# Rotary embedding in a two-block network: the half swap by ScalarE copies out of PSUM or by DMA transfers inside SBUF

## The chip, the cores and the metric

The kernel runs on one core of one Trainium2 chip. The metric is the time of one execution on the device, in microseconds. A core has five engines that run side by side, each through its own queue in order: TensorE (PE; its weight loads are listed as PEld), VectorE (DVE), ScalarE (ACT), GpSimd (POOL) and SyncE (SP). SBUF is the core's working memory of 128 partitions, PSUM the memory that TensorE writes its sums to, and 16 DMA engines move data to and within SBUF.

## What is computed

The reference is a network of two blocks over 256 tokens of 1,024 features, batch 1. The first block has two attention layers, one with compressed, selected and windowed keys and one with dilated windows; the second block has a gated feed-forward part, a mixer with a gated delta rule and a convolution, and a second feed-forward part. All is float32. What matters here is the rotary embedding, which is applied to heads of 64 features in both attention layers:

```python
def rope(x):
    T = x.shape[1]
    half = x.shape[-1] // 2
    inv = ROPE_THETA ** (-jnp.arange(half, dtype=jnp.float32) / half)
    ang = jnp.arange(T, dtype=jnp.float32)[:, None] * inv[None, :]
    cos = jnp.cos(ang)[None, :, None, :]
    sin = jnp.sin(ang)[None, :, None, :]
    xf = x.astype(jnp.float32)
    x1, x2 = xf[..., :half], xf[..., half:]
    return jnp.concatenate([x1 * cos - x2 * sin, x2 * cos + x1 * sin], axis=-1).astype(x.dtype)
```

Each output needs the feature of its own place and the feature of the other half of its head.

## The kernel before

Activations lie transposed: features on the partitions, 128 at a time (a feature tile), and the 256 tokens along the row. A feature tile holds two heads of 64, so the halves of the heads are four blocks of 32 partitions, and to change the halves means that block 0 goes to block 1, 1 to 0, 2 to 3 and 3 to 2.

All products with weights stream the weights once from memory. A unit of up to 1 MB comes by one DMA from SP into one of three buffers named raw (`fetch`, line 234). To keep float32 accuracy at the speed of a reduced format, it is cut into a high part `hi` (a cast on ACT, line 216) and a low part `lo` (a subtraction on DVE, line 219), and PE makes three passes for each pair of tiles. The raw buffer is free again when the subtraction has read it. Beside this, `ada_gen` makes the modulation sums of later layers on DVE (line 371) out of further units of raw, at a rate that the code sets per stage.

A group of 512 output columns fills two PSUM banks, each with two feature tiles of 256 tokens. PSUM has three banks tagged g, two s, two t and one o. When a group is complete, an evacuation function takes the banks out. For q and k these are:

- `ev_kv` and `ev_q` in the first attention layer (lines 754 and 774). `ev_kv` copies the bank to a temporary on ACT (line 760) and calls `rope` once; `ev_q` scales the bank into `qp` on ACT (line 777) and calls `rope` for each of four banks. What comes out is cut into high and low parts (lines 766, 783, 784) for the scores.
- `ev_r` in the second attention layer (line 988). It scales the bank into a temporary on ACT (line 991) and calls `rope`, for four banks of q and four of k. The results go straight to `qr` and the block-diagonal `kr`, from which `scores` (line 1011) starts as soon as the k of four head pairs is there.

So `rope` runs 13 times. It gets the scaled values twice: `src` in SBUF, and the bank `ps` in PSUM with the factor `scale`. Four ACT instructions (line 677), one for each block of 32 partitions, read the neighbouring block of the bank, scale it and write it to a temporary `t2`; DVE multiplies that with the signed sine (line 678); POOL multiplies `src` with the cosine (line 680); DVE adds both (line 682). The temporaries [128, 512] (tag w5) have four buffers for all uses. In the second layer a call holds three: the scaled copy, `t2` and the cosine product. In the first layer it holds `t2`, the cosine product and the result.

Within an engine the order of instructions is fixed when the program is built: a planner goes through the program with its own estimate of durations, takes what is ready by priority, and places the waits between engines. At run time each engine works through its list in that order.

Of the kernel before, what the change touches and what calls it, by code (L numbers as in the profile page):

```python
# [14 lines left out]
PSUM = bass.MemoryType.PSUM  # L15
# [97 lines left out]
FILL = [[1, 2, 0, 0, 0, 0, 0], [1, 1, 2, 0, 0, 2, 2]]  # units of the queued products at the seven points of a half of the delta rule  # L113


def pack_small(inp):
    """Vectors as columns: element q of row r of the row-major [rows, 128] view goes to (q, r)."""
# [9 lines left out]
def pack_w2(inp):  # L127
    """Second compression matrices, their 64 columns twice: [128, k/v, k tile, 128]."""
    two = [np.concatenate([np.asarray(inp[f"nsa_c{n}_w2"])[0].reshape(2, 128, 64)] * 2, 2).transpose(1, 0, 2) for n in "kv"]
    return np.ascontiguousarray(np.stack(two, 1))  # L130
# [10 lines left out]
def pack_units(inp, plan):  # L141
    """Weights in the order and layout in which the kernel reads them, 128 partitions by up to 2048 words a unit."""
# [15 lines left out]
class Net:  # L158
# [20 lines left out]
    # ------------------------------------------------------------ helpers  # L179
# [12 lines left out]
    def touch(self, t):  # L192
        """Slots of a tag are given out in the order of the first writes: this takes one now for a tile filled later."""
        self.nc.gpsimd.memset(t[:, 0:1].bitcast(F32), 0.0)
        return t
# [35 lines left out]
    # ------------------------------------------------------------ weights  # L231
# [25 lines left out]
    def group(self, ncol, orient="A", tags="ggg", tail=False, wide=False):  # L257
        """Accumulators for at most 512 columns of a weight: banks, place of each tile in them, tiles, first matmuls"""
# [9 lines left out]
    def direct(self, G, ws, x, k0, nkt):  # L268
        """Adds the float32 products of feature tiles k0 on with the weights as they came."""
# [15 lines left out]
    def part(self, G, ws, act, k0, nkt, early=False, late=False, passes=((0, 0), (1, 0), (0, 1))):  # L285
        """Adds the products of feature tiles k0 on, whose weights are ws, to a group."""
# [27 lines left out]
    def fill(self, n):  # L314
        """The next n units of the products that wait to be put between the steps of others."""
# [4 lines left out]
    def until(self, gen):  # L320
        """All units of a product that waits."""
# [3 lines left out]
    def gemm_steps(self, wsrc, cols, act, evac, orient="A", tail=False, last=None, x=None, dset=()):  # L325
        """cols = list of (c0, width) forming one group of at most 512 columns of the weight.
        A: evac(bank list, each [128, 2, 256] = feature tiles); B: evac([bank per token tile])."""
# [31 lines left out]
    # ------------------------------------------------------------ background modulation sums  # L359
# [30 lines left out]
    # ------------------------------------------------------------ setup  # L390
    def setup(self):
# [20 lines left out]
        # modulation jobs in the order of their need  # L412
# [23 lines left out]
    def silu_row(self, row, pe=False):  # L436
        """silu of a vector, in every partition"""
# [20 lines left out]
    # ------------------------------------------------------------ norm  # L458
    def stats(self, xT, k0, n, two=False):
        """Adds feature tiles k0 to k0 + n of x to the sums of squares per token; two: also to those weighted by self.og."""  # L460
# [22 lines left out]
    def rstd(self):  # L483
        """1 / rms over features, in every partition: PSUM [128, 256]."""
# [6 lines left out]
    def spread(self, r, tag):  # L491
        """A value per token, [128, 2], in every partition: PSUM [128, 256]."""
# [5 lines left out]
    def normed(self, xT):  # L498
        """hi/lo of rms_norm(x) * g * (1 + scale) + shift, per feature tile, and the first products."""
# [5 lines left out]
    def ahead(self, g, mod, j, g0=None):  # L505
        """The factor and the shift of the norm that follows a projection, known before its sums of squares are."""
# [8 lines left out]
    def unscaled(self):  # L515
        """The first columns behind a norm: (r * a * x + s) @ w = r * ((a * x) @ w) + s @ w, so that the product with w
        doesn't wait for r.  s goes along as two more tokens, its high and its low part."""
# [15 lines left out]
    def rescaled(self):  # L533
        """The feature tiles of these columns, [128, 512] for two."""
# [1129 lines left out]
```

## Time and profile before

| | us |
|---|---|
| median of the timed runs | 1123.79 |
| lowest and highest of them | 1122.24, 1124.45 |
| span of the profiled execution | 1131.5 |
| PE busy | 1077.3 |
| DVE busy | 861.2 |
| ACT busy | 616.7 |
| POOL busy | 64.4 |

The profile is of one execution, recorded instruction by instruction; its span is from the first to the last instruction. Busy times of an engine count its instructions and not the issue of DMAs. PE's matmuls are pipelined, so a busy PE is not PE at its peak. Where an engine sat idle, the profile names what ended the wait. An idle engine costs time only if something that sets the end waits for it.

### The profile page before, as it was taken

What the parts mean: (1) busy time and instruction counts of PE and PEld (TensorE: products, weight loads), DVE (VectorE), ACT (ScalarE), POOL (GpSimd) and SP (SyncE); (2) the same over time, 40 slices, a digit from 0 to 9 for tenths busy, and PEclk for the clock granted to TensorE, in tenths of its full rate; (3) what the DMA queues carried; (4) which work ended last, traced back from release to release, by engine and by line L of the source; (5) the groups of instructions that cost most, each with busy time, mean ns of one, the idle gap of its engine ahead of it and who ended that gap; (6) DMA issues with size and microseconds to landing.
All of it is one profiled execution on the core that took longest, in us unless ns stands there. A gap on an engine that the chain in (4) does not pass through costs nothing.

```text
span 1131.5 us, 20245 instructions
## 1 busy us (share of the span) xinstructions
PE 1077.3 (95%) x8145; PEld 1003.1 (89%) x8145; DVE 861.2 (76%) x1571; ACT 616.7 (55%) x1190; POOL 64.4 (6%) x70
## 2 busy tenths in 40 slices
PE   5889999989999999999999799999999999999997
PEld 4868776977789899999989679998999999999997
DVE  7885887799999898887689789568866667565543
ACT  3482676688765644444388246644644556444442
POOL 0030000222000000000000020002000000000000
PEclk9998999999999999999999989999999999999998
DMA  8855455657768487878743523263346544555451
GB/s 332 330 202 198 149 172 201 247 207 258 259 240 292 178 316 266 310 271 326 261 153 139 147 76 114 81 220 113 117 145 227 184 152 176 195 178 177 169 185 38
DMA packets 33423, 226.34 MB, mean 200 GB/s; under 512 B 3681, under 2 KB 3937, under 8 KB 7346
## 3 DMA queue, kind: packets, MB, share of 16 engines
q1 hardware_dynamic: 32914, 224.20, 55.0%
q8 instruction: 64, 1.05, 0.4%
q10 hardware_dynamic: 288, 0.52, 0.1%
q0 software_dynamic: 128, 0.33, 0.1%
q14 instruction: 29, 0.24, 0.1%
HBM read 223.73 MB, written 1.31 MB: 199 GB/s over the span
## 4 chain that ended last, share of the span: by engine, by line
issue 35%; PE 20%; DVE 6%; DMA 3%; ACT 2%; POOL 1%; SPq 0%; POOLq 0%; DVEq 0%; ACTq 0%
PE g L206 12%; PE s L206 5%; DMA b<-dr 2%; DVE w L1218 1%; DVE lo L219 1%; PE t L206 1%; DMA raw<-in_ws_dram 1%; PE o L206 1%; ACT hi L216 1%; DVE xt L1368 0%; POOL rrq L1279 0%; PE t L213 0%; DVE xs L1369 0%; DVE b L1447 0%; DVE b L1456 0%
## 5 line engine op out<-in xcount | busy, mean ns | idle before, releaser
L206 PE MATMUL g<-b,hi 128*128 128x256 f32 (+2 forms) x3696 | 692.2, 286 | 9.1 <-ACT b L586 7.3
L206 PEld LDWEIGHTS g<-b,hi 128*128 128x128 f32 (+1 forms) x3696 | 578.7, 191 | 16.5 <-ACT b L586 9.2
L206 PE MATMUL g<-b,lo 128*128 128x256 f32 (+2 forms) x1848 | 520.1, 286 | 8.6 <-DVE lo L219 8.5
L216 ACT CAST hi<-raw 128x1024 fp32r<-128x1024 f32 (+2 forms) x302 | 280.1, 953 | 228.6 <-PE g L206 124.6
L219 DVE TENSOR_TENSOR lo<-raw,hi 128x1024 fp32r<-128x1024 f32 (+2 forms) x302 | 328.5, 1110 | 90.7 <-ACT hi L216 90.3
L206 PEld LDWEIGHTS g<-b,lo 128*128 128x128 f32 (+1 forms) x1848 | 348.8, 191 | 12.6 <-DVE lo L219 10.3
L371 DVE SCALAR_TENSOR_TENSOR raw<-raw,scrow 128x1024 f32<-128x1024 f32 x120 | 147.1, 1247 | 4.0 <-DMA raw<-in_ws_dram 3.9
L206 PE MATMUL s<-b,hi 128*128 128x256 f32 (+1 forms) x288 | 63.8, 288 | 2.3 <-ACT w L546 2.3
L206 PE MATMUL g<-b,raw 128*128 128x256 f32 x208 | 52.3, 385 | 0.0
L206 PE MATMUL s<-b,b 128*128 128x128 f32 (+2 forms) x224 | 49.0, 342 | 3.0 <-DVE b L682 1.5
L206 PEld LDWEIGHTS s<-b,hi 128*128 128x128 f32 x288 | 49.4, 193 | 2.5 <-ACT w L546 2.5
L1218 DVE SCALAR_TENSOR_TENSOR w<-pad,u,w 128x256 f32<-128x256 f32 x96 | 41.7, 481 | 2.3 <-ACT w L1213 2.2
L206 PEld LDWEIGHTS g<-b,raw 128*128 128x128 f32 x208 | 37.2, 191 | 5.0 <-issue 0.5
L206 PE MATMUL s<-b,lo 128*128 128x256 f32 (+1 forms) x144 | 40.4, 288 | 0.0
L206 PEld LDWEIGHTS s<-b,b 128*128 128x128 f32 x224 | 30.2, 191 | 8.2 <-ACT b L1028 3.2
L206 PE MATMUL t<-b,hi 128*128 128x256 f32 x160 | 37.4, 280 | 0.0
L1129 DVE TENSOR_TENSOR w<-w,g 128x512 f32<-128x512 f32 (+1 forms) x21 | 14.2, 675 | 24.8 <-PE g L206 24.8
L925 ACT ACTIVATE p<-s,mxs 128x256 f32<-128x256 f32 (+1 forms) x64 | 26.4, 420 | 9.5 <-DVE mxs L923 7.0
L488 POOL TENSOR_TENSOR rcol<-rcol,u 128x2 f32<-128x2 f32 x5 | 3.5, 702 | 489.4 <-ACT rcol L487 489.4
L1127 ACT ACTIVATE w<-g 128x512 f32<-128x512 f32 (+1 forms) x21 | 12.3, 587 | 33.0 <-PE g L206 33.0
L206 PE MATMUL g<-hi,b 128*128 128x512 f32 (+1 forms) x96 | 28.2, 372 | 1.8 <-ACT hi L216 1.6
L206 PEld LDWEIGHTS o<-u,w 128*128 128x128 f32 x224 | 27.4, 192 | 1.2 <-issue 0.6
(321 smaller groups left out, 1323.8 us busy)
## 6 DMA issues: line engine op xcount, KB each, us to landing
raw<-in_ws_dram SPq DMA_DIRECT2D x202, 1024.0 KB, 4.8
b<-dr SPq DMA_DIRECT2D x8, 512.0 KB
raw<-in_ws_dram SPq DMA_DIRECT2D x4, 512.0 KB, 3.8
raw<-in_ws_dram SPq DMA_DIRECT2D x2, 608.0 KB, 3.9
b<-in_xT_dram SPq DMA_DIRECT2D x1, 1024.0 KB
u<-in_consts_dram SPq DMA_DIRECT2D x2, 384.0 KB
u<-in_consts_dram SPq DMA_DIRECT2D x1, 527.0 KB
u<-in_consts_dram SPq DMA_DIRECT2D x2, 256.0 KB, 5.9
```

The source lines that it names most:

```text
L206: i = self.nc.tensor.matmul(out, lhsT=lhsT, rhs=rhs, start=start, stop=stop, skip_group_check=True)
L216: i = self.nc.scalar.copy(hi, src)
L219: self.nc.vector.tensor_tensor(lo, src, hi, op=ALU.subtract)
L371: nc.vector.scalar_tensor_tensor(r, r, 1.0, sc, op0=ALU.mult, op1=ALU.mult, accum_out=mod[:, n:n + 1])
L488: nc.gpsimd.tensor_tensor(r, r, self.mhalf[:, 0:2], op=ALU.pow)
L925: nc.scalar.activation(p[:, br], sv[:, br], AF.Exp, bias=mx[:, q, br:br + 1], accum_out=den[:, q, br:br + 1])
L1127: nc.scalar.activation(t, gb, AF.Tanh, scale=0.5)
L1129: nc.vector.tensor_tensor(t, t, ub, op=ALU.mult)
L1218: nc.vector.scalar_tensor_tensor(dst, fl(pad[:, o:o + 256]), taps[i], dst, op0=ALU.mult, op1=ALU.add)
```

## The change

In `rope` the four ACT copies out of PSUM are replaced by four DMA transfers from `src`, the scaled values in SBUF. They are issued on ACT's queue, and each moves 32 partitions by 512 float32 values (64 KB). The parameters `ps` and `scale` stay in the signature and are no longer used. All other lines of the diff are comments and docstrings that became empty lines.

```diff
         t2 = v(self.w([128, 512], tag="w5", bufs=4))
         for k in range(4):
-            nc.scalar.activation(t2[32 * k:32 * k + 32], ps[32 * (k ^ 1):32 * (k ^ 1) + 32], AF.Copy, scale=scale)
+            nc.scalar.dma_start(t2[32 * k:32 * k + 32], src[32 * (k ^ 1):32 * (k ^ 1) + 32])
         nc.vector.tensor_tensor(t2, t2, bc("ropes"), op=ALU.mult)
```

With it `t2` waits for `src` to be written and for its buffer, the bank `ps` is read by one ACT instruction (in `ev_kv` by that one and the copies of line 759), and line 678 waits for four transfers. ACT still issues the step, from its own queue, and SP's queue has nothing new in it.

## Rows read from the trace of the kernel before

**Rows 1.** The page's first part: busy us, share of the span, instructions.
```profile
PE 1077.3 (95%) x8145; PEld 1003.1 (89%) x8145; DVE 861.2 (76%) x1571; ACT 616.7 (55%) x1190; POOL 64.4 (6%) x70
```
**Rows 2.** By stretch: PE, PEld, DVE, ACT, POOL busy (instructions), clock, DMA share, GB/s.
```profile
50.00:92.00 42.00, 37.06 (x234) 29.64 (x234) 34.33 (x55) 32.10 (x59) 9.94 (x7) 0.93 0.58 209
225.00:300.00 75.00, 69.12 (x429) 57.00 (x429) 70.25 (x101) 62.13 (x140) 13.51 (x8) 1.00 0.65 226
92.00:225.00 133.00, 130.12 (x808) 104.22 (x807) 100.02 (x242) 80.21 (x238) 5.72 (x7) 0.96 0.54 195
300.00:570.00 270.00, 268.17 (x2201) 261.26 (x2199) 227.67 (x393) 135.85 (x202) 2.57 (x6) 1.00 0.74 274
```
**Rows 3.** Waits in 225 to 300: who for whom, us, times, longest.
```profile
DVE w L678 <- ACT w L677: 3.4, 5, 1.6
...
PE g L206 <- ACT w L677: 1.1, 2, 1.0
```
**Rows 4.** Waits in 50 to 92 us.
```profile
PE o L206 <- DMA raw<-in_ws_dram: 2.0, 2, 1.6
...
PE g L206 <- ACT hi L216: 1.6, 1, 1.6
...
DVE w L678 <- ACT w L677: 0.5, 1, 0.5
```
**Rows 5.** Line 677: count, ns min/median/max, first and last start.
```profile
L677 ACT ACTIVATE w<-g x36: 588/590/593, 54.1 to 280.3; 32x512 f32<-32x512 f32 x36
...
L677 ACT ACTIVATE w<-w x4: 625/628/632, 232.1 to 234.0; 32x512 f32<-32x512 f32 x4
```
**Rows 6.** Line 621, the stores at the end: issue ns, and landing.
```profile
L621 SPq DMA_DIRECT2D out_dram<-b x2: 338/345/352, 1126.5 to 1127.7; - x2
L621 ACTq DMA_DIRECT2D out_dram<-b x2: 338/356/374, 1127.1 to 1128.3; - x2
...
DMA to landing us min/median/max: 2.1/2.2/2.2
```
**Rows 7.** DMA issues with size and us to landing; then issue ns of line 1352.
```profile
raw<-in_ws_dram SPq DMA_DIRECT2D x202, 1024.0 KB, 4.8
w<-in_w_dram SPq DMA_DIRECT2D x1, 256.0 KB, 4.2
...
L1352 SPq DMA_DIRECT2D b<-dr x8: 567/572/697, 619.3 to 740.1; - x8
```
**Rows 8.** DVE's groups in 225 to 300: busy us, mean ns, idle before.
```profile
L219 DVE TENSOR_TENSOR lo<-raw,hi 128x1024 fp32r<-128x1024 f32 (+1 forms) x20 | 23.8, 1223 | 0.7 <-ACT hi L216 0.7
L371 DVE SCALAR_TENSOR_TENSOR raw<-raw,scrow 128x1024 f32<-128x1024 f32 x14 | 19.1, 1376 | 0.0
L1025 DVE TENSOR_REDUCE dmx<-s 128x2 f32<-128x256 f32 (+1 forms) x16 | 8.6, 553 | 0.1
```
**Rows 9.** ACT in order of time, first layer: start us, us.
```profile
69.11 1.79 ACT L677 ACTIVATE w<-s 32x512 f32<-32x512 f32 x3
70.93 0.95 ACT L216 CAST hi<-raw 128x912 fp32r<-128x912 f32 x1
```
**Rows 10.** PE in order of time; in brackets idle before it, and its releaser.
```profile
71.93 0.55 PE L206 MATMUL g<-hi,b 128*128 128x304 f32 x2 [1.63 <-ACT hi L216]
```
**Rows 11.** Busy time by stretch, 65 to 80 us (columns as in rows 2).
```profile
65.00:70.00 5.00, 3.42 (x17) 1.68 (x16) 4.18 (x6) 4.82 (x9) 1.57 (x2) 1.00 0.76 261
70.00:75.00 5.00, 2.98 (x10) 1.14 (x8) 4.12 (x5) 4.84 (x9) 2.00 (x1) 0.81 0.69 249
75.00:80.00 5.00, 5.00 (x28) 4.02 (x27) 3.62 (x8) 4.56 (x8) 1.29 (x1) 0.85 0.39 118
```
**Rows 12.** ACT in order of time, second layer, from one scaled copy to the next.
```profile
239.72 0.60 ACT L991 ACTIVATE w<-g 128x512 f32<-128x512 f32 x1
240.35 2.39 ACT L677 ACTIVATE w<-g 32x512 f32<-32x512 f32 x4
242.77 0.60 ACT L991 ACTIVATE w<-g 128x512 f32<-128x512 f32 x1
```

## The prediction

> **What bounds the kernel now.** I read the page's busy shares first. TensorE (PE) is busy 95% of the profiled span, DVE 76%, ACT 55% [rows 1]. So the time is PE's work plus PE's gaps, and the 31 us that ACT spends on these copies are worth nothing unless a gap of PE, or of an engine that PE waits for, hangs on them. The next view is busy time by stretch [rows 2]. The 13 calls of rope lie in two stretches: five in 50 to 92 us (one for k, four for q of the first layer) and eight in 225 to 300 us (four for q, four for k of the second). There PE has 4.9 and 5.9 us of gaps. In the second stretch DVE is busy 70.25 of 75 us, so it is nearly the bound beside PE; in the first, DVE is at 34.3 and ACT at 32.1 of 42. After each stretch PE is close to full (130.1 of 133, 268.2 of 270), so what is lost or won in a rope stretch is mostly carried to the end.
>
> The third view is the waits of both stretches. What the four copies of line 677 hold up today is little: DVE's product with the sine (line 678) waits 3.4 us in five places of the second stretch and 0.5 us in the first, and PE waits 1.1 us for the copies to give back an accumulator bank [rows 3, 4]. The longest gap of PE in the first stretch that has ACT behind it is 1.6 us for a weight cast of line 216 [rows 4].
>
> **What is removed.** 52 ScalarE copies: 36 out of the g banks at 0.59 us, 12 out of other banks at the same 0.59, and 4 from SBUF at 0.63 [rows 5] (the first and the last of four groups); 52 x 0.59 = 31 us of ACT. A group of four reads 2.40 us in order of time [rows 12], so a rope loses 2.40 us of ACT.
>
> **What is added.** 52 transfers of 32 partitions by 2,048 bytes, 64 KB each, issued on ACT's queue. The only DMAs issued there now are two stores of 256 KB at 0.356 us of ACT's sequencer; the cheapest of the four stores took 0.34 on SP [rows 6], and the dearest group of issues, b<-dr, 0.57 [rows 7]. I take 0.356: 4 x 0.356 = 1.42 us a rope. ACT keeps 2.40 - 1.42 = 0.98 us a rope, 12.7 us in all (bounds 2.40 - 4 x 0.57 = 0.1 to 2.40 - 4 x 0.34 = 1.0 a rope).
>
> **How late the swapped halves are.** Today they are there 2.4 us after the scaled copy. A transfer's time to landing is not shown for this size, nor for SBUF to SBUF. From below: 2.1 us, the stores on the quiet queue at the end [rows 6]. From above: 4.2 us for a 256 KB load inside the first rope stretch, 4.8 for a full 1 MB load [rows 7]. The DMA engines are 58% and 65% busy in the two stretches [rows 2], so I weigh quiet and busy by 0.35 and 0.65: 0.35 x 2.1 + 0.65 x 4.2 = 3.5 us. The last of four is issued 3 x 0.356 = 1.07 us after the first, so the halves are there after 4.6 us (bounds 1.07 + 2.1 = 3.2 and 1.07 + 4.8 = 5.9): 2.2 us later than now.
>
> The Trainium skill, "DMA: Bandwidth & Descriptors", section "Queues, rings and completion order", says that a DMA engine takes turns between its queues packet by packet, so these transfers would not stand behind a whole weight load. By that, a rope's transfers wait only for about their own volume of weights: 768 KB more take a load 4.8 - 2.1 = 2.7 us longer [rows 6, 7], so 256 KB take 0.9, the halves would come after 3.2 + 0.9 = 4.1 us (an estimate by that rule), and the sum below would be +0.6 in place of +1.4 us. No row here shows two loaded queues side by side.
>
> **Who waits.** Behind line 678 DVE's whole in-order queue is held: the subtractions of line 219 that give PE its low weights, the modulation sums of line 371, the score maxima of line 1025. That queue also has what can cover the wait: 23.8 + 19.1 + 8.6 = 51.5 us of such work in the second stretch [rows 8], 6.4 us a rope. The order is made at build time, and today it leaves uncovered 3.4 of 8 x 2.4 = 19.2 us (18%) in the second stretch and 0.5 of 12 us (4%) in the first. I keep these shares for the longer latency: 0.18 x 8 x 4.6 = 6.6 and 0.04 x 5 x 4.6 = 0.9, together 7.5 us of DVE waiting in place of 3.9: **+3.6 us**. If everything is covered it is -3.9; if 40% of the second stretch is not, 14.7 + 0.9 - 3.9 = +11.7.
>
> **What PE wins.** The bank is free after the first copy and not after five ACT instructions, so the 1.1 us that PE waits for line 677 go [rows 3]. The cast that PE waits 1.63 us for starts at 70.93, right behind copies of line 677 that run from 69.11 [rows 9, 10]; three ropes' savings (3 x 0.98) are ahead of it, so that wait goes too, and the weight load of the compression is next in line. Together **-2.7 us** (bounds 0 and -2.7, and a little of clock: the gaps from 65 to 75 us are followed by a granted clock of 0.81 and 0.85 up to 80 us, part of that time at 1.2 instead of 2.4 GHz; were it all given back it would be 5 x 0.19 + 5 x 0.15 = 1.7 us [rows 11]).
>
> **What the weight loads lose.** A rope moves 256 KB, a quarter of a 1 MB load, so by the load's time it can set a load back by up to 4.8 / 4 = 1.2 us. PE waits for loads only at the compression, 2.0 us in two places [rows 4]: 0 to 2.4 us. The engines are idle 35 to 42% of the time, so most of it finds room; I take **+0.5 us**. SP's own queue is passed by nothing, since ACT issues the transfers; POOL's product with the cosine (line 680) reads the same source as before and is unmoved.
>
> **Sum.** +3.6 - 2.7 + 0.5 = +1.4 us. It is made on a profiled execution with a span of 1131.5 us; the timed runs have a median of 1123.79 (1122.24 to 1124.45), 7.7 us under that span, so I carry the difference over: 1123.79 + 1.4 = **1125.2 us**. With U for the uncovered DVE wait the net is U - 3.9 - 2.7 + 0.5 = U - 6.1.
>
> **The rivals.** About 0.2% (2.25 us) is what a measurement of this kernel can tell from no change. By the line above, U under 3.85 us (0.30 a rope) is faster, over 8.35 us (0.64 a rope) slower.
>
> Slower, by DVE: the order puts line 678 where it thinks the halves have landed, and beside weight loads they have not. At 40% uncovered in the second stretch, where DVE has under 5 us of slack, the net is 15.6 - 6.1 = +9.5 us, 1133. For it: DVE is 94% busy there, and the DMA engines are busier (65%) than where the 4.2 us landing was (58%). Against it: 51.5 us of other DVE work to hide 37 us of latency in.
>
> Slower, by ACT's queue: the pool of [128, 512] temporaries has four buffers, and a rope of the second layer holds three (scaled copy, swapped, cosine product). The swapped tile of the second rope of a pair must take the buffer of the first rope's scaled copy, which the transfers now read until they land. ACT reaches its issue 0.60 + 1.42 = 2.0 us after the first copy's end and would stand until 4.6: 2.6 us, for four pairs 10.3 us, with casts of line 216 behind it [rows 12]. ACT's slack (12.9 us plus 7.8 saved) takes most; if one of the holds reaches PE and the wins are lost too, 1.4 + 2.7 + 2.6 = +6.7, 1130.5.
>
> Slower, by transfers one behind the other: four landings in a row take 4 x 2.1 = 8.4 us, U = 0.18 x 8 x 8.4 + 0.04 x 5 x 8.4 = 13.8, net +7.7, 1131.5. Against it: the two stores on ACT's queue and two on SP's each landed in 2.1 to 2.2 us with issues close behind each other [rows 6]. The Trainium skill's DMA page, section "Rules for kernel authors", says that transfers to disjoint parts of the partitions serialize and that one large transfer should be used; these four are such a case. By that rule the change is slower; the store rows speak against a full serialization.
>
> Faster: the order covers the latency. With half of today's wait left, U = 2 and the net is -4.1, 1119.7; with none, -6.1, 1117.7. For it: ACT is busy 91% or more from 65 to 80 us, where the first layer's ropes are [rows 11], and banks come free earlier. Against: ACT bounds only that short piece.
>
> **Chances.** Even (U between 3.85 and 8.35) 0.36, my forecast. Slower 0.38: by DVE 0.24, by ACT's queue 0.08, by serial transfers 0.06. Faster 0.26. So the single likeliest case is no change, with 1121.5 to 1126 as its own range, while the slower cases together weigh slightly more. The range for 8 in 10 goes from 1117 (all covered) to 1137 (half the second stretch uncovered: 0.5 x 8 x 4.6 + 0.9 - 6.1 = +13.2).
>
> **What the profile after would show.** Right: line 677 as 52 DMA issues on ACT's queue at 0.33 to 0.4 us, landing in 3 to 4 us; DVE's wait before line 678 at 7 to 8 us, now for a DMA; no PE wait for line 677; the cast behind 70.93 earlier by over a microsecond. Wrong: landing beyond 5 us or in steps (serial); ACT idle before an issue of line 677 for a buffer; DVE's wait over 9 us with PE gaps for line 219 behind it; or that wait under 3 us. A different order of the work after the ropes, which I can't foresee from this trace, would blur all of it.

## The result

The changed kernel takes 1142.94 us (median; 1140.66 to 1151.23) beside 1123.79 for the kernel before: a ratio of 1.0166, 95% interval 1.0135 to 1.0197, or 19 us more. The profiled execution has a span of 1149.4 us beside 1131.5. The forecast was 1125.2, with a range from 1117 to 1137.

First the page of the changed kernel: ACT's busy time, then the transfers with their size and the median time from issue to landing. (The profile has the landing of only 7 of the 52, 5 of the first kind and 2 of the second, so these medians are of a few.)

```profile
PE 1080.1 (94%) x8145; PEld 1003.2 (87%) x8145; DVE 861.3 (75%) x1571; ACT 584.6 (51%) x1138; POOL 64.5 (6%) x70
...
w<-w ACTq DMA_DIRECT2D x36, 64.0 KB, 4.1
...
w<-b ACTq DMA_DIRECT2D x16, 64.0 KB, 6.7
```

ACT lost 32 us of work against [rows 1], as foretold, and the kernel lost 19. To see where, I cut the profile at two places that every version has: the *first stretch* runs from the first instruction of line 760 to the first reduction of line 545 (it holds the first attention layer), the *second stretch* from there to the last instruction of line 1095 (the scores of the second layer). Busy time of both, kernel before (from:to length, PE, PEld, DVE, ACT, POOL with counts, granted clock, DMA share, GB/s):

```profile
53.50:223.10 169.60, 161.78 (x1009) 128.72 (x1009) 129.12 (x286) 108.72 (x290) 15.66 (x14) 0.96 0.55 196
223.10:336.50 113.40, 107.00 (x707) 89.67 (x707) 106.16 (x193) 88.03 (x187) 13.51 (x8) 1.00 0.67 239
```

and the changed kernel:

```profile
53.60:230.70 177.10, 161.04 (x1009) 127.24 (x1008) 130.46 (x285) 96.44 (x270) 15.01 (x14) 0.95 0.55 195
230.70:357.60 126.90, 112.78 (x726) 92.85 (x725) 106.89 (x199) 70.21 (x158) 14.01 (x8) 0.99 0.67 237
```

The first stretch is 7.5 us longer, the second 13.5; what follows gives back some 2 us by line 597 and 1 us after that. DVE does the same work in the second stretch (106.2 and 106.9 us), but it idles 126.9 - 106.9 = 20.0 us there in place of 113.4 - 106.2 = 7.2. (19 more matmuls, of the stage behind, fall before the second stretch's end.)

What DVE, ACT and SP waited for in the changed kernel: first stretch, second stretch, then SP over the whole span (engine, line, releaser: us in total, times, longest).

```profile
ACT b L783 <- DVE w L682: 12.9, 3, 7.2
DVE w L678 <- DMA w<-b: 9.1, 2, 5.7
...
DVE w L678 <- DMA w<-w: 2.8, 1, 2.8
...
DVE w L678 <- DMA w<-w: 12.1, 7, 3.4
...
ACT hi L216 <- DMA raw<-in_ws_dram: 10.6, 5, 5.7
ACT w L991 <- DVE b L682: 10.4, 3, 5.3
...
ACT w L449 <- DVE b L682: 6.8, 1, 6.8
...
SPq L234 <- DMA w<-w: 14.1, 3, 7.3
```

DVE stands 24.0 us before the product with the sine (9.1 + 2.8 + 12.1), where it stood 3.9 [rows 3, 4]. In the first layer ACT stands behind it, for the results (line 783, 12.9 us). In the second it is idle 17.2 us before lines 991 and 449; the view puts that down to sums of line 682, and the order of time below reads otherwise. And SP's weight loads wait 14.1 us for landings of the transfers, a wait that the kernel before does not have at all. All of it lies in the second stretch; in the first SP waits 0.7 us for a transfer.

One place of the first layer in order of time, DVE (start, us, engine, line; in brackets idle before it, and its releaser):

```profile
80.05 0.57 DVE L825 TENSOR_TENSOR ke<-kcp,u 128x240 f32<-128x240 f32 x1
86.30 0.69 DVE L678 TENSOR_TENSOR w<-w,u 128x512 f32<-128x512 f32 x1 [5.68 <-DMA w<-b]
86.90 0.40 DVE L837 TENSOR_TENSOR hidt<-hidt,o 32x256 f32<-32x256 f32 x1
```

The four semaphores that this product waits for are those of the transfers issued at 71.01, 76.34, 76.89 and 77.54; it starts at 86.30, and PE's transposes for the compression wait 7.0 us for line 837 (1.3 in the kernel before), which stands behind it in DVE's queue. ACT at the same time:

```profile
79.00 0.51 ACTq L677 DMA_DIRECT2D w<-b  x1
...
87.94 0.62 ACT L783 CAST b<-w 64x512 fp32r<-64x512 f32 x1 [7.19 <-DVE w L682]
87.95 1.16 ACTq L677 DMA_DIRECT2D w<-b  x2
```

The next rope has its first transfer issued at 79.00, and its others only behind a cast that waits for the late rope's sum. In the second layer, ACT and then DVE:

```profile
252.86 2.71 ACTq L677 DMA_DIRECT2D w<-w  x4
255.68 0.60 ACT L991 ACTIVATE w<-g 128x512 f32<-128x512 f32 x1 [2.56 <-DVE b L682]
...
261.48 2.44 ACTq L677 DMA_DIRECT2D w<-w  x4
263.96 0.64 ACT L449 ACTIVATE w<-scrow 128x512 f32<-128x512 f32 x1 [6.75 <-DVE b L682]
```

```profile
252.89 0.69 DVE L678 TENSOR_TENSOR w<-w,u 128x512 f32<-128x512 f32 x1 [0.69 <-DMA w<-w]
...
261.50 0.69 DVE L678 TENSOR_TENSOR w<-w,u 128x512 f32<-128x512 f32 x1 [3.03 <-DMA w<-w]
...
267.05 0.69 DVE L678 TENSOR_TENSOR w<-w,u 128x512 f32<-128x512 f32 x1 [0.79 <-DMA w<-w]
```

Four issues take 2.44 us of ACT's queue, as long as the four copies did [rows 12], and they do not follow the scaled copy at once. The copy that starts at 255.68 has its transfers issued from 261.48, the moment at which the landing of the rope before releases DVE's product. The trace shows ACT waiting there for the semaphores of that rope's four transfers: `t2` takes the buffer of that rope's scaled copy, and the transfers read it until they land. So ACT's idle time before lines 991 and 449 is mostly the issues and this stand, and the ropes of the second layer go one behind the other (us; a product starts when its halves have landed, except the fifth, which did not wait):

| rope | scaled copy ends | issues start | product starts |
|---|---|---|---|
| 1 | 239.7 | 239.7 to 241.6 | 245.3 |
| 2 | 242.8 | 245.4 to 247.2 | 252.9 |
| 3 | 248.5 | 252.9 to 255.0 | 261.5 |
| 4 | 256.3 | 261.5 to 263.3 | 267.1 |
| 5 | 268.2 | 270.1 to 274.1 | 278.3 |
| 6 | 275.9 | 278.6 to 282.5 | 289.9 |
| 7 | 284.9 | 290.0 to 291.9 | 298.2 |
| 8 | 293.2 | 298.2 to 300.1 | 305.4 |

In the kernel before these products start 2.5 to 4.1 us behind the end of the scaled copy, here 5.6 us (the first) and 10.1 to 14.0. And where the transfers stay, seen in two pieces of the DMA view, one behind four issues beside a weight load, one behind four issues in a quiet moment (q1 carries SP's loads, q10 ACT's transfers: packets, MB, share of the 16 engines):

```profile
q1 hardware_dynamic: 133, 0.96, 100.1%
...
w<-w ACTq DMA_DIRECT2D x4, 64.0 KB
```

```profile
q10 hardware_dynamic: 104, 0.15, 21.9%
q1 hardware_dynamic: 15, 0.05, 4.6%
...
w<-w ACTq DMA_DIRECT2D x4, 64.0 KB, 2.2
```

From 245.3 to 247.9 us loads have the engines to themselves and no packet of the transfers moves. From 289.9 to 292.6 104 of their packets move, and the one transfer whose landing is recorded lands in 2.2 us; the last of that rope still comes at 298.2, with a load issued meanwhile.

### The profile page after: what moved, and what is told of

Read it like the earlier page. It is cut to its first block, busy times and chain, and to the rows that moved or that the text cites. A ratio compares the mean times of both kernels' runs of the same rounds, so it can differ in the third digit from the quotient of the medians.

```text
span 1149.4 us, 20311 instructions
## 1 busy us (share of the span) xinstructions
PE 1080.1 (94%) x8145; PEld 1003.2 (87%) x8145; DVE 861.3 (75%) x1571; ACT 584.6 (51%) x1138; POOL 64.5 (6%) x70
## 4 chain that ended last, share of the span: by engine, by line
issue 35%; PE 19%; DVE 6%; DMA 3%; ACT 2%; POOL 1%; SPq 0%; POOLq 0%; DVEq 0%; ACTq 0%
PE g L206 12%; PE s L206 5%; DMA b<-dr 2%; DVE w L1218 1%; DVE lo L219 1%; PE t L206 1%; PE o L206 1%; DMA raw<-in_ws_dram 1%; ACT hi L216 1%; DVE xt L1368 0%; POOL rrq L1279 0%; PE t L213 0%; DVE xs L1369 0%; DVE b L1447 0%; DVE b L1456 0%
## 5 line engine op out<-in xcount | busy, mean ns | idle before, releaser
L206 PEld LDWEIGHTS g<-b,lo 128*128 128x128 f32 (+1 forms) x1848 | 350.2, 191 | 15.1 <-DVE lo L219 12.9
L206 PE MATMUL s<-b,b 128*128 128x128 f32 (+2 forms) x224 | 51.6, 351 | 8.9 <-ACT p L925 3.6
L206 PEld LDWEIGHTS s<-b,b 128*128 128x128 f32 x224 | 31.4, 195 | 13.5 <-ACT p L925 4.4
L206 PEld LDWEIGHTS t<-b,hi 128*128 128x128 f32 x160 | 28.4, 188 | 0.0
```

Source lines behind the costliest of these rows:

```text
L206: i = self.nc.tensor.matmul(out, lhsT=lhsT, rhs=rhs, start=start, stop=stop, skip_group_check=True)
```

## The experiments

The theories, as they came up: **late halves** (DVE stands for the landing, and others behind it), **mutual waits** on ScalarE's queue (as the program is built, the DMAs of SP and ACT take turns on eight completion semaphores, the same eight for both in the trace, and each waits until the one before it on its semaphore has landed; GpSimd's have eight others), **issue time** on ACT, **traffic**, **held buffers**, and last **the planner's order**. Line numbers in rows of an experiment are shifted by up to three; the text names the lines of the kernel before.

**e1_first and e2_second: one layer at a time.**

```
         for k in range(4):
-            nc.scalar.dma_start(t2[...], src[...])
+            if self.layer == "n":      # e2: !=
+                nc.scalar.dma_start(t2[...], src[...])
+            else:
+                nc.scalar.activation(t2[...], ps[...], AF.Copy, scale=scale)
```

> The transfers stand only in the five calls of the first layer; the eight of the second layer copy out of PSUM as before. In the two traces the first layer's part ends 7.6 us later with the change. If each layer pays for its own calls, whatever the mechanism, this kernel is 6 to 9 us slower than before (1130 to 1133 us). If the loss came from a different order of all later work and not from the calls, it is anywhere else, and the first layer's and the second layer's kernels don't add up to the 19 us of the whole change.

> The transfers stand only in the eight calls of the second layer. By the traces that stretch loses 13 us and the stages behind it give 2 to 3 back: 9 to 13 us slower than before (1133 to 1137 us), and with the first layer's kernel the sum is 19 us. If the second layer only suffers because the first hands it a late weight stream, it is under 5 us.

Measured: 1.0081 (1.0045 to 1.0118) and 1.0071 (1.0036 to 1.0107). Each layer costs half, and the halves add up to the whole (1.5% and 1.7%). The profiles agree on the place: with e1 the second stretch is 113.7 us, with e2 the first is 167.2.

**e3_unread: issued as in the change, but nobody waits for the landing.**

```
+        sp = v(self.t(self.dram, [128, 512], tag="rd", bufs=4))
         for k in range(4):
-            nc.scalar.dma_start(t2[...], src[...])
-        nc.vector.tensor_tensor(t2, t2, bc("ropes"), op=ALU.mult)
+            nc.scalar.dma_start(sp[...], src[...])
+        nc.vector.tensor_tensor(t2, src, bc("ropes"), op=ALU.mult)
```

> All 52 transfers are issued as in the change, on ACT's queue, but into a scratch tensor in device memory that nobody reads, and the sine product reads the unswapped values (the swap is left out of the result). Issue, volume and the shared DMA semaphores stay; DVE's wait for the landing and the hold on the temporaries go. If the loss is DVE's wait for late landings, with the temporaries that they hold, this is within 3 us of the kernel with no swap at all (e4). If it is the weight loads on SP that wait for semaphores which the transfers hold, 8 us or more of the loss stay over that kernel, and SP still waits over 8 us for these transfers.

Measured: 1.0122 (1.0069 to 1.0176). First stretch 173.1 us, second 118.3: without any standing of DVE half of the first stretch's price is still there and a third of the second's, and by the medians three quarters of the whole. Late halves alone don't explain the change. (The transfers go to device memory here, and one hold stays: a scaled copy's buffer is taken until the transfers have read it.)

**e4_floor: no swap at all** (neither copies nor transfers; the product reads the scaled copy).

> Neither copies nor transfers: the sine product reads the unswapped values (the swap is left out of the result). It shows what a swap that costs nothing would give, the gain on which the change could have counted. By the sum of the prediction (no wait for line 677, ACT 31 us freer) 4 to 7 us faster than before, 1117 to 1120 us; if ACT's time is covered altogether, within 2 us of before.

Measured: 1.0035 (0.9999 to 1.0070); stretches 167.2 and 113.8 us. This miss says most about what was to be had: 31 us of ACT taken away altogether bring nothing that can be measured.

**e5_pool_queue: GpSimd issues the transfers.** `nc.scalar.dma_start` becomes `nc.gpsimd.dma_start`.

> The 52 transfers are issued by GpSimd in place of ScalarE; nothing else differs from the changed kernel. In that one, the weight loads of SyncE waited 14.8 us for landings of the transfers, and VectorE stood 24.0 us before the product with the sine. Theory A, shared semaphores: the transfers of ScalarE and the weight loads of SyncE take turns on the same eight completion semaphores and so wait for each other; GpSimd's transfers have others, so SyncE's waits on them are 0, and the time falls from 1143 to 1126-1132. Theory B, late halves: the landing is set by the weights' packets, whoever issues; VectorE still stands 18 us or more and the time stays at 1138-1146. Theory C, issue time: ScalarE no longer spends 0.61 us on each transfer (32 us in all); it would fall to 1128-1134 with SyncE's waits gone as well, so A and C are not told apart by this run alone.

Measured: 1.0123 (1.0074 to 1.0172). SP no longer waits for any transfer. The first stretch is at 169.0 us, as before the change; the second stays at 127.4, with DVE standing 9.3 us in it. All 52 landings are in this profile: 1.8 to 7.4 us after the issue, median 4.7. The two layers have different causes.

**e6_pool_unread.** By a slip the queue was not changed in this kernel, so what ran is e3_unread once more, and its expectation was tested only by e10.

> The transfers go from GpSimd to a scratch that nobody reads, and the product with the sine reads the scaled copy as it is: the change of places is left out. Run e3_unread was the same on ScalarE's queue and was 1.2% slower than the kernel before, although nobody waited for a landing. With GpSimd's queue neither the halves, nor the shared semaphores, nor ScalarE's issue time are left, only the transfers' traffic. Theory A or C (semaphores, issue): 1119-1127, as the kernel without any swap. A rival, that the traffic itself slows the weight loads: the loss of e3_unread stays, 1135-1140.

Measured: 1.0140 (1.0105 to 1.0176), stretches 172.4 and 118.3 us: e3 repeats within a microsecond. ACT's waits of this profile have two kinds of stand for transfers. The scaled copies (line 991) wait for their own buffer, which an earlier rope's transfers still read; the casts (line 783) stand behind transfers that wait for their turn on a semaphore.

```profile
ACT w L992 <- DMA rd<-w: 7.2, 2, 3.9
...
ACT b L784 <- DMA rd<-b: 4.9, 2, 3.7
```

**e7_one_transfer: one transfer of 128 partitions a rope**, `nc.scalar.dma_start(t2, src)`, without the change of places.

> One transfer of the whole copy (128 partitions, 256 KB) on ScalarE's queue in place of four of 64 KB; the change of places is left out. The same bytes behind the same weight loads, one issue and one semaphore in place of four. Theory A, shared semaphores: a quarter of the waits of SyncE's loads on them, 4 us in place of 15, and 1129-1134. Theory B, late halves: the landing is as late, VectorE stands 18-24 us, 1138-1146. Theory C, issue time: 13 issues in place of 52, 1130-1135.

Measured: 1.0119 (1.0069 to 1.0169). The one transfer is issued in 0.47 us, and SP waits for none. The profile has the landing of two of the 13 (2.7 and 3.2 us). In the seven places where DVE stands for one, it is released 4.3 to 8.8 us after the issue (median 6.4; in the ten places of the change 5.5 to 15.3 us after the first of the four issues, median 7.6). DVE stands 19.4 us before its product. The first stretch falls to 171.4 us, the second is 125.4.

**e8_own_buffers: four buffers of their own for the swapped halves of the second layer.**

```
-        t2 = v(self.w([128, 512], tag="w5", bufs=4))
+        t2 = v(self.w([128, 512], tag="w5", bufs=4) if self.layer == "n"
+               else self.t(self.sp, [128, 512], tag="rt", bufs=4))
```

> The changed kernel, with four buffers of their own for the swapped halves in the second layer (in the first they stay in the shared ring of four). Theory D, held buffers: the ring's temporaries are held over late landings and ScalarE stands for them (24 us in the second layer's trace), which is most of that layer's +13 us; with own buffers the time falls to 1132-1136. Theory A or B: the halves land as late and SyncE's loads wait as long; 1140-1145.

Measured: 1.0236 (1.0211 to 1.0261), slower than the change itself. In the second layer ACT's scaled copies and casts stand 14.3 us for landings, and SP stands 15.3 us for transfers. The scaled copies still share four buffers, and the transfers hold them until they have read them: the hold was moved and not taken away, so held buffers are not settled by this run.

**e9_more_vector_work: the kernel before, with two additions more ahead of each rope's sum.**

```
+        for p, d in dst * (2 // len(dst)):
+            nc.vector.tensor_tensor(d, t2[p], t2[p], op=ALU.add)
         for p, d in dst:
             nc.vector.tensor_tensor(d, t1[p], t2[p], op=ALU.add)
```

> The kernel before, with its four ScalarE copies, and two additions more on VectorE ahead of each rope's last addition (their result is overwritten): some 1.3 us of work more a rope, 8 ropes in the second layer (10.4 us), 5 in the first (6.5 us). No transfer is added. In the kernel before VectorE is busy 72.3 of the 77.2 us from 223.1 to 300.3. Theory E, VectorE is the bound of the second layer's stretch, so that whatever holds it there is paid one for one: that stretch is 7-11 us longer (10.4 less at most the 4 us in which it stood before), the first layer's 0-4 us, and the time 1131-1138. The rival, which is what the prediction went by (TensorE sets the pace and VectorE's waits of a few us cost a part of themselves): under 4 us in all, 1123-1128.

Measured: 1.0133 (1.0080 to 1.0186). Both stretches of its profile:

```profile
53.40:223.80 170.40, 157.74 (x1009) 124.27 (x1008) 137.03 (x296) 108.52 (x290) 14.14 (x14) 0.97 0.54 196
223.80:352.00 128.20, 111.62 (x726) 93.25 (x725) 119.00 (x215) 89.64 (x189) 14.37 (x8) 0.99 0.59 217
```

DVE got 7.9 us more work in the first stretch (137.0 against 129.1), which became 0.8 us longer; and 12.8 us more in the second (119.0 against 106.2), which became 14.8 us longer, above the 7 to 11 expected. In the second layer DVE's time is the path, in the first it is not.

**e10_gpsimd_unread: e3 with GpSimd's queue**, so that only the traffic is left.

> What e6_pool_unread was meant to be: the transfers into a scratch that nobody reads are issued by GpSimd; the product with the sine reads the scaled copy as it is, so the change of places is left out. Neither late halves, nor shared semaphores with SyncE's loads, nor issue time on ScalarE; only the traffic is left. Theory A or C (semaphores or issue are what e3_unread lost): within 4 us of the kernel before, 1120-1128, and the second layer's stretch (from the first reduction of line 545 to the last instruction of line 1095; 113.4 us before, 118.3 in e3_unread) is at 113-115. The rival, the traffic: 117-119 us there and 1133-1140.

Measured: 1.0032 (1.0004 to 1.0059); stretches 166.1 and 116.3 us. With the traffic alone the kernel stands where it stands without any swap (e4).

**e11_gpsimd_copies: GpSimd copies from the scaled copy**, `nc.gpsimd.tensor_copy(t2[...], src[...])`, no transfers.

> No transfer: four GpSimd copies from the scaled copy in SBUF to the swapped halves in place of ScalarE's four out of PSUM. ScalarE loses its 31 us of copies, no queue is touched, and the halves are as late as GpSimd is slow: the product with the cosine on it takes some 1.3 us for 128x512, so that four copies of 32 rows, if each takes 0.6-1.2 us, end 2.4-5 us behind the scaled copy. Theory E (VectorE's standing is the price): it stands about as long as in the kernel before if the copies take 0.6 us, 1120-1127, and 10 us more at 1.2 us, 1130-1136. If the transfers' traffic or semaphores were the price: 1118-1126 either way.

Measured: 1.0203 (1.0152 to 1.0254). A copy of 32 rows takes GpSimd a median of 0.98 us (0.60 to 1.51; ACT 0.59 [rows 5]), four of them 3.9, and DVE stands 10.5 us for them. No transfer is in it, and the second stretch is 127.3 us all the same: 5 us of that is DVE's own work, which reads longer there (111.2 against 106.2), the rest its idle time (16.1 against 7.2). The time, 1147.7 us, is above the 1130 to 1136 expected for slow copies.

**e12_split_loads: each weight load in two.**

```
-        self.nc.sync.dma_start(raw[:, :width], self.A["ws"][len(self.plan), :, :width])
+        for c in range(0, width, 1024):
+            self.nc.sync.dma_start(raw[:, c:min(c + 1024, width)], self.A["ws"][...])
```

> The changed kernel with each 1 MB weight load split into two of half the columns. A step of the explanation: the transfers land late because they stand behind a whole weight load on the DMA engines. If so, their landing falls from a median of 5.8 us to 4-5 and VectorE's waits before the product with the sine from 24.0 us to 12-18. If the landing is the transfers' own latency, it stays at 5.5-6. The whole time says less, since twice as many loads take turns on SyncE's semaphores: 1135-1155.

Measured: 1.0254 (1.0195 to 1.0314). The landing has a median of 5.1 us (2.0 to 8.3, of 23 transfers), DVE stands 10.6 us before the product for transfers, 5.5 more in one place that the profile puts down to a load, and 30.3 us for the split loads at line 371 (1.9 in the change). Too much moves at once; whether the transfers stand behind whole loads is not settled by it.

**e13_products_later and e15_later_gpsimd.** In the second layer the products of four ropes come behind the last scaled copy of the four, with eight own buffers; e15 also has GpSimd's queue. The core of the edit:

```
+        if self.layer == "d":
+            self.later.append((dst, src, t2))
+            return
...
+        for dst, src, t2 in self.later:
+            i = nc.vector.tensor_tensor(t2, t2, bc("ropes"), op=ALU.mult)
+            self.tc.add_manual_dep(i.ins, self.last_ev.ins.name, NOSYNC, reason="later")
+            nc.gpsimd.tensor_tensor(src, src, bc("ropec"), op=ALU.mult)
+            for p, d in dst:
+                nc.vector.tensor_tensor(d, src[p], t2[p], op=ALU.add)
```

> The changed kernel, in whose second layer the scaled copies and the swapped halves of four ropes (two of q, two of k) have eight buffers of their own, and the four products with the sine and their additions come after the last scaled copy of the four, so that q's stand some 4 to 10 us of other work later in VectorE's order; the product with the cosine is made in place. ScalarE's transfers are as they were. Theory E (VectorE is full in that stretch, and its standing is the price there): it stands 2-7 us before the product with the sine in the second layer instead of 12.1, the stretch from the first reduction of line 545 to the last instruction of line 1095 falls from 126.9 to 117-122 us, and the time to 1131-1137. The rival, that the waits of SyncE's loads and ScalarE's transfers for each other are the price there: 124-129 us and 1140-1148.

> e13_products_later with all 52 transfers issued by GpSimd: neither the standing nor the mutual waits are left, beside what k's late halves still hold. If the two causes are all there is: within 5 us of the kernel before (1121-1130), with 114-119 us in the second layer's stretch. If something third is in it, the traffic or GpSimd's issue time: over 1133.

Measured: 1.0225 (1.0202 to 1.0247) and 1.0083 (1.0051 to 1.0116). DVE stands only 5.2 and 2.8 us before the product in the second stretch, but the stretches are 129.3 and 123.8 us, and DVE idles 20.4 and 14.5 us in them. The standing was moved, not removed: DVE idles in other places, in e13 before line 371 (4.1 us for a weight load and 7.2 for nothing that the profile names). e13 is a miss for late halves as I had put it, and e15 with 1135.2 us is over the 1133 above which its expectation put something third. Between the two, with the same edit, the queue (and the order that the planner chose for it) makes 1.4%.

**e14_gpsimd_first: the kernel before, with transfers in the first layer only, issued by GpSimd.**

```
+            if self.layer == "n":
+                nc.gpsimd.dma_start(t2[...], src[...])
+            else:
                 nc.scalar.activation(t2[...], ps[...], AF.Copy, scale=scale)
```

> The kernel before, in whose first layer alone the halves change places by transfers, issued by GpSimd instead of ScalarE (e1_first: the same on ScalarE's queue, +0.81%). The halves land as late. Theory A (in the first layer the price is the mutual waits of ScalarE's transfers and SyncE's loads): 0-4 us over the kernel before, and 165-171 us from line 760 to line 545 (169.6 before, 173.5 in e1_first). The rival, late halves in the first layer too: 8-10 us over it, 173-178 us.

Measured: 1.0005 (0.9982 to 1.0028); first stretch 166.7 us. DVE's waits in it:

```profile
DVE w L681 <- DMA w<-b: 5.8, 2, 4.5
DVE w L681 <- DMA w<-w: 2.6, 1, 2.6
```

DVE stands 8.4 us for late halves and it costs nothing. The same transfers on ACT's queue (e1, DVE standing 9.0 us) cost 0.8%. SP's waits are not that difference: in e1's first stretch SP waits 0.5 us for a transfer.

**e16_changed_again: the changed kernel, beside e13 to e15.**

> The changed kernel again, beside the other three on the same chip: 1.4-1.9% over the kernel before, 1140-1146; its second layer's stretch within 4 us of 126.9 and the first layer's within 4 us of 177.1. Where they differ by more, single profiles can't be read to some us.

Measured: 1.0182 (1.0156 to 1.0208), stretches 174.1 and 127.0 us, DVE standing 21.4 us. Single profiles of a kernel differ by some 3 us in the first stretch, by less in the second.

**e17_work_behind: e9's work behind the sums**, `nc.vector.tensor_tensor(t2, t2, bc("ropes"), op=ALU.mult)` twice after the loop of line 681, so that no rope waits for its own.

> The kernel before, with two products more on VectorE behind each rope's last addition, into a temporary that is no longer read (e9_more_vector_work had as much ahead of it): no rope waits for its own additional work. Theory E, VectorE's time as such is the price of the second layer's stretch: that stretch is 7-12 us longer than 113.4, as in e9 (128.2), and the time 1131-1138. The rival, it is the lateness of q and k that is paid and VectorE has room behind them: 113-117 us and 1123-1128.

Measured: 1.0164 (1.0111 to 1.0216). DVE has 13.5 us more work in the second stretch and it is 15.4 us longer (128.8); 7.9 more in the first, 2.2 longer. The 15.4 is above the 7 to 12 expected. It is DVE's time as such that is paid in the second layer, not the place of a rope in it.

**e18_order_of_before: the changed kernel in the old order.** Every instruction has its counterpart in the kernel before, so each engine's list could be fixed to that kernel's list.

```
+        mine = [i for i in traced if str(i.engine) == "EngineType." + name]
...
+                tc.add_manual_dep(mine[at], mine[last].name, NOSYNC, reason="order")
```

> The changed kernel with every engine's instructions in exactly the order of the kernel before; each transfer stands where the copy stood that it replaces. Theory, the price is the transfers' own (late halves, VectorE held, the waits on ScalarE's queue): the order of before puts the products with the sine no later than the changed kernel's own, so VectorE stands as long or longer (24-40 us in all instead of 24.0) and the time is 1140-1155. The rival, the price is that of the planner's other order: 1121-1130, as the kernel before.

Measured: 1.0264 (1.0204 to 1.0325), and both stretches are longer than the change's own:

```profile
55.10:235.50 180.40, 163.15 (x1009) 129.98 (x1008) 129.81 (x286) 96.91 (x270) 14.99 (x14) 0.94 0.54 193
235.50:368.70 133.20, 113.39 (x708) 95.21 (x707) 103.75 (x193) 69.03 (x154) 12.83 (x8) 0.92 0.61 218
```

```profile
DVE w L678 <- DMA w<-w: 29.5, 8, 6.9
...
DVE w L678 <- DMA w<-b: 8.1, 3, 4.8
```

The planner's other order is not the price. It won back a third: in the old order DVE stands 37.5 us instead of 24.0.

Together, for the transfers:

| | ratio | first stretch | second stretch | DVE idle in the second |
|---|---|---|---|---|
| kernel before | 1 | 169.6 | 113.4 | 7.2 |
| ACT's queue, read (the change, e16) | 1.0166, 1.0182 | 177.1, 174.1 | 126.9, 127.0 | 20.0, 21.0 |
| ACT's queue, unread (e3, e6) | 1.0122, 1.0140 | 173.1, 172.4 | 118.3, 118.3 | 11.0, 11.1 |
| GpSimd's queue, read (e5) | 1.0123 | 169.0 | 127.4 | 20.3 |
| GpSimd's queue, unread (e10) | 1.0032 | 166.1 | 116.3 | 8.4 |
| no swap (e4) | 1.0035 | 167.2 | 113.8 | 5.4 |

In the second layer reading the halves makes 9 to 11 us (126.9 - 118.3 and 127.4 - 116.3), the queue 2 at most. In the first layer the queue makes 5 to 8 us (174.1 and 177.1 against 169.0; 173 against 166), reading 1 to 5, not clear of the 3 us by which two profiles of one kernel differ. Each version has the order that the planner chose for it, so a few us between two of them may be the order's. None of the versions beats the kernel before.

## Why the prediction was wrong

**The step that failed is how late the halves are.** I had them 4.6 us behind the scaled copy, with bounds of 3.2 and 5.9. In the second layer of the change they were 5.6 us behind it in the first rope and 10.1 to 14.0 in the six others whose landing DVE waited for. All three parts of that sum were too small. I let ACT issue right behind the copy; from the second rope on its first issue came 1.9 to 5.2 us later, in most of them at the very moment when the rope before had landed. I let the last issue start 1.07 us after the first; it was 1.8 to 3.9. And from the last issue to the release of the product I had 3.5 us (2.1 to 4.8); it was 3.7 to 7.4.

**The share failed too, but not alone.** I foretold U = 7.5 us of DVE standing; it was 24.0. In the second layer 12.1 us stood where 6.6 were foretold, of 62 us from the first issues to the products: 19%, and I had 18%, so there the miss is the lateness. (The planner's order was another one, so that is no proof of the share.) In the first layer 11.9 us stood where 0.9 were foretold: 21% of 57 us, and I had 4%. In the old order itself (e18) the share does not hold in either layer: 24.2 of 48 us and 13.4 of 40 us. Nor does an order hide a fixed length: before the change it hid 15.8 / 8 = 2.0 and 11.5 / 5 = 2.3 us a rope; with e18's lateness of 6.0 and 8.0 us from the first issue, U would be 8 x (6.0 - 2.0) + 5 x (8.0 - 2.3) = 60 us, and it was 37.5. I had read the 51.5 us of other work as cover for the whole; but a queue in order covers only by what stands between the issue and the product.

**The price of U** came out by luck: by the prediction's own line, U - 6.1 = 17.9 gives 1141.7, and 1142.9 was measured; for e18 it gives 31.4, and 30.8 was measured. But 2.7 of the 6.1 us are a win that is not there, and the line fails elsewhere: it gives 15.3 us for the change repeated (e16; measured 21.2), 17.8 for e8 (26.8) and 8.2 for e13 (25.9). In the second layer e9 and e17 show that DVE is the path, as the 94% of [rows 2] said and as the rival "slower by DVE" put it. Its 40% (14.7 us) is near the 12.1 us of that layer by number only: it was 40% of 37 us, and this is 19% of 62. In the first layer standing can cost nothing (e14), and what costs is ACT's queue; one stand of the change lies on the path there, the 5.7 us ahead of line 837, for which PE waits 7.0 us (4.5 in e1, 3.1 in e14).

**Issue.** 0.356 us was taken from stores of 256 KB [rows 6]; these transfers took a median of 0.61, outside the bound of 0.57. Four issues are 2.44 us where four copies were 2.40, so ACT's queue won nothing.

**PE's win, -2.7 us,** is not there. Run e4 frees ACT of the copies for nothing and is at +0.35% (-0.01 to 0.70).

**Weight loads, +0.5 us.** I priced the volume, and for the volume alone it was right (e10 is at +0.32%, e4 without any transfer at +0.35%). What I missed is what a queue adds. From e10 to e3 and e6, whose edits differ only in the queue, the ratio goes from 1.003 to 1.012 and 1.014. DMAs of two engines can wait for each other: 14.1 us of SP waiting for landings of ACT's transfers, and ACT in turn standing before its issues (e6). But those 14.1 us lie in the second layer, where the queue makes 2 us at most; in the first, where it makes 5 to 8, SP waits 0.7 us in the change and 0.5 in e1. Since ACT's issues take no longer than the copies, issue time alone can't be it either. What is left is ACT's own order, in which transfers stand behind casts that wait for the rope before (87.94 above); it was not tried apart.

**The landing.** The Trainium skill, "DMA: Bandwidth & Descriptors", section "Queues, rings and completion order", has the engines take turns by packets, and I read it as a wait for no more than a rope's own volume. The rows here differ from that reading: in 245.3 to 247.9 us 0.96 MB of loads pass ahead of four issued transfers, and the recorded landings go from 2.2 us in a quiet moment to 7.5 beside loads. The same section gives 9 to 17 descriptors as typical for a packet; a load has 128 rows over 16 engines, 8 for each, so by it a load's whole share of an engine can pass ahead. That agrees with the rows, but e12 could not confirm it.

**The other rivals.** "By ACT's queue" (held temporaries) had the mechanism of the second layer: the first issue came late in seven of eight ropes, 27 us in all (part of it filled with ACT's other work) where I had put 10.3 us of standing, and I gave it 0.08. That, landings beyond 5 us and a DVE wait over 9 us were three of my own signs of being wrong. What the hold costs is not shown: own buffers for the swapped halves don't help (e8), but the scaled copies stayed held. "One behind the other": the same page, section "Rules for kernel authors", advises one transfer over 128 partitions in place of several over parts; the trace agrees in direction (e7: DVE released 6.4 us after the issue against 7.6 after the first of four, both medians), and still e7 is 1.2% slower than the copies. That the order changed, which I could not foresee, made the change better and not worse (e18).

**What stays open:** what of ACT's queue costs in the first layer; what the held buffers cost in the second, since no run has the products in place with own buffers for scaled copies and halves; why DVE's idle time in the second layer stays at 20 us when its standing before the product is taken away by a later place (e13); and whether a transfer passes a weight load only as a whole.

## What to carry to other kernels

When a copy is replaced by a transfer, ask first when the transfer can be issued. It reads its source until it lands, so a buffer that the copies did not touch (they read PSUM) is held for the whole landing, and what needs that buffer next stands in its engine's queue: here the next rope's transfers, so that one late rope made the next one later. Only then add issues and landing. How much of the lateness an order covers could not be taken from the old profile, neither as a share nor as a length. On an engine that is 94% busy in a stretch more work is paid about one for one (e9, e17), while the 31 us freed on an engine with room were worth nothing. And ask what a transfer stands behind in the queue that issues it: here the same transfers cost nothing in the first layer from GpSimd's queue and 0.8% from ScalarE's.

## What the hardware showed that was not expected

- The issue of a transfer inside SBUF took 0.61 us for 32 partitions by 2 KB on ACT (0.51 to 1.84), 0.47 for 128 partitions (e7), 0.50 on GpSimd (e5); the stores of [rows 6] took 0.34 to 0.37.
- The same 64 KB landed in 2.2 us in a quiet moment and in up to 7.5 us beside weight loads (7 landings of the change); from GpSimd's queue, with all 52 landings recorded, in 1.8 to 7.4 us, median 4.7 (e5). One transfer of 256 KB landed in 2.7 and 3.2 us where the landing is recorded; DVE was released 4.3 to 8.8 us after the issue where it stood for one (e7).
- SyncE's and ScalarE's DMAs share eight completion semaphores as this program is built, so SyncE's weight loads waited 14.1 us for landings of ScalarE's transfers; GpSimd's transfers have eight others, and there SyncE waited for none (e5).
- GpSimd took 0.98 us (0.60 to 1.51) for a copy of 32x512 for which ACT takes 0.59.
